# One PSUM tile or two for a head's attention scores, and a new fixed order of TensorE in the attention loop

## The chip, the cores and the metric

The kernel runs on one core of one Trainium2 chip. The metric is the device time of one execution in microseconds (us). A core has five engines that this text calls by the profile's names: PE (TensorE: matrix products and transposes; PEld is its weight load), DVE (VectorE), ACT (ScalarE), POOL (GpSimd) and SP (which issues DMAs here). In this kernel PE writes its results to tiles in PSUM, and DVE and ACT read them from there. [...] The engines work side by side and wait for one another by semaphores.

## What is computed

One layer of a hybrid block over 2048 latent tokens and 256 context tokens of width 1024: a modulated norm, one input projection, then two groups of heads side by side, an output projection, and a feed-forward part. The change lies in the stage in which both head groups are worked on. What it computes:

```python
keys = jnp.concatenate([kc, kx], axis=1)          # 256 + 2048 = 2304 keys
def block(q):                                     # 128 queries, 2 x 4 heads of 64
    s = jnp.einsum('bqkgd,bnkd->bkgqn', q, keys).astype(jnp.float32) * scale
    p = jax.nn.softmax(s, axis=-1)
    return jnp.einsum('bkgqn,bnkd->bqkgd', p.astype(vals.dtype), vals)
...
def step(S, inp):                                 # gated linear recurrence, 4 heads, two directions
    ...
    A = jnp.einsum('bhtk,bhsk,bhtsk->bhts', qc, kc, decay)
    o = jnp.einsum('bhts,bhsv->bhtv', A, vc) + jnp.einsum('bhtk,bhkv->bhtv', qc * jnp.exp(b), S)
```

## The kernel before

The kernel has three large stages: the norm and the input projection; the attention heads with the recurrence woven in; the output projection and the feed-forward part. Only the second stage is touched. PE's instructions there are issued in the order in which the program writes them (a manual schedule for PE alone, from the line `border.enter_context`). The instructions of DVE, ACT and POOL are put in order by the compiler's planner, which runs through the program on a model of the chip.

**Items.** The loop `for item in work` runs over 64 items: 2 key groups, 16 blocks of 128 queries, 2 pairs of heads. An item is a `Pair`: two heads of one block. Items overlap: while the scores of `cur` are made, the transposes and products of `prev` (the item before) are done, and `done` (the one before that) is finished.

**A head's scores.** `scores(hh, i)` handles one of two segments of the 2304 keys: segment 0 has 1536 keys, segment 1 has 768. PE writes the segment into PSUM (L814: 6 products of 512 columns for segment 0, 4 for segment 1, since each is the sum of two halves). DVE takes the minimum over each segment (L816; the queries carry the negated scale, so a minimum stands for the maximum), and over the two minima (L818). With segment 1, ACT then makes the exponentials of both segments into the SBUF tile `pr` (L822), each with a sum read out behind it. Before the change both segments lie in one PSUM tile `s_all` of 2560 columns, five banks, made once (L791) and written by every head.

**Transposes.** `transposes(k2)` (k2 from 0 to 8) turns two 128-column pieces of `pr` for both heads on PE (L831, four transposes) into a one-bank tile `pt` of the pool `ps_t2`, and copies it to the SBUF tile `pf`. The copy is on DVE (L835) for the k2 in `EV_DVE`, otherwise on ACT (L837). The pool has two banks.

**Products.** `products()` multiplies the nine `pf` tiles with the values (L844, 36 products, into one more tile of `ps_t2`), and ACT copies the result to `ot` (L848). `finish()` transposes `ot` on PE (L859, tile `pof`, also of `ps_t2`), and DVE divides by the sums (L861, L862, L864). POOL adds two halves (L866) and SP stores the block.

**The recurrence.** `other()` advances a generator `recurrence()`, which keeps two units of the other head group going in turn. A step is mostly one level of a tree: PE writes `pa` (L638), DVE merges it into `A` (L641), POOL makes the next `M`, `C` and `Q` (L650, L653, L662, L664), ACT copies parts (L656, L657), DVE makes the next `T` (L669). Other steps are `pd` (L627), transposes `pk` (L678) with copies on ACT (L680), `psf` and `psb` (L685, L697) with DVE's `S` (L692), and `po` (L728 to L730). All PSUM of the recurrence comes from `ps_h`, a pool of one bank. `STEPS / SLOTS` of a step is owed for each call, so that some calls advance nothing.

**The order.** One item issues its work to PE as `ORDER` says: -1 and -2 are segments 0 and 1 of the item's first head, -3 and -4 those of its second head; a positive number is so many transposes of `prev`; 0 is one call of `other()`. After the entry that leaves five transposes to do, `done.finish()` is called. `prev.products()` ends the item.

Of the kernel before, what the change touches and what calls it, by code (L numbers as in the profile page):

```python
# [9 lines left out]
F32 = mybir.dt.float32  # L10
F32R = mybir.dt.float32r
I32 = mybir.dt.int32
AF = mybir.ActivationFunctionType
ALU = mybir.AluOpType
AX = mybir.AxisListType

P = 128
# [25 lines left out]
DVE_MOD = (2, 5)  # L43
N_T, N_H = 2, 1
LIVE = 2
EV_DVE = (2, 5)
QI = WOE = "gpsimd"
STEPS = 4.4


ORDER = (-1, 2, 0, -2, 2, 0, 2, 0, 1, 0, -3, 2, -4, 0)
SLOTS = ORDER.count(0)

C_Q, C_K, C_HQ, C_I, C_FF, C_FB, C_G = 0, 512, 768, 1280, 1792, 2304, 2816
# [2 lines left out]
def rows_bcast(ap, n=P):  # L57

    return bass.AP(tensor=ap.tensor, offset=ap.offset, ap=[[0, n], [1, ap.size()]])
# [12 lines left out]
def block_kernel(ctx: ExitStack, tc: tile.TileContext, a: dict, out: bass.AP, dbg=None):  # L72
    nc = tc.nc
# [3 lines left out]
    def pool(stack, name, bufs=1, space=None, side=None):  # L77
        kw = dict(name=name, bufs=bufs, reuse_waits="tile", side=side)
        if space is not None:
            kw["space"] = space  # L80
        return stack.enter_context(tc.tile_pool(**kw))
# [67 lines left out]
    with ExitStack() as st:  # L149
# [36 lines left out]
        for r in range(2):  # L186
            for which in range(2):
                ks = slice(which * KT, (which + 1) * KT)
                nc.vector.tensor_tensor(modc[:, 2 * r + 1 - which, :], pcol[:, ks, r], bcol[:, ks],
                                        op=ALU.add)  # L190
# [21 lines left out]
    with ExitStack() as st:  # L212
# [39 lines left out]
        with ExitStack() as p1:  # L252
            ps_x = pool(p1, "ps_x", 4, PSUM)
            xh = pool(p1, "xh", 2)
            for gr in list(range(1, NTOK // 256)) + [0]:
# [7 lines left out]
                o = (gr - 1) % 2 * 256 if gr else 0  # L263
# [18 lines left out]
                for kk in range(KT // 2):  # L282
# [6 lines left out]
                    hh = xh.tile([P, 512], F32, tag="h", name=f"h{gr}_{kk}")  # L289
# [239 lines left out]
        for b in range(4):  # L529
            for gen, n in ((kv, 4 if b < 3 else 6), (hq, 2)):  # L530
                if b == 3 and gen is hq:
                    next(kv, 0)
                    w = load_w(steps[2][2])
# [6 lines left out]
        for i in range(2, len(steps)):  # L540
            f, c, _ = steps[i]
# [19 lines left out]
            w = wn  # L561
# [8 lines left out]
    with ExitStack() as st:  # L570
# [4 lines left out]
        op = pool(st, "op", 1, side="right")  # L575
# [3 lines left out]
        ps_s2 = pool(hst, "ps_s2", 1, PSUM)  # L579
# [208 lines left out]
        SEG = [(0, 1536), (1536, NTOK - 1536)]  # L788
        NSEG = len(SEG)
        NKT = NTOK // P  # L790
        s_all = ps_s2.tile([P, 2560], F32, name="s_all")  # L791

        class Pair:

# [7 lines left out]
            def scores(self, hh, i):  # L802


                nm = f"{self.nm}_{hh}"
                if i == 0:
                    self.negs.append(sm.tile([P, NSEG + 1], F32, tag="neg", name=f"neg{nm}"))
                neg = self.negs[hh]
                k0, n = SEG[i]
                for o, w in MM:  # L810
                    if not k0 <= o < k0 + n:
                        continue
                    for half in range(2):
                        nc.tensor.matmul(s_all[:, o:o + w], self.qs[:, hh, self.item[2], half, :],  # L814
                                         self.kv[0][:, o:o + w], start=(half == 0), stop=(half == 1))
                nc.vector.tensor_reduce(neg[:, i:i + 1], s_all[:, k0:k0 + n], axis=AX.X, op=ALU.min)  # L816
                if i == NSEG - 1:
                    nc.vector.tensor_reduce(neg[:, NSEG:], neg[:, :NSEG], axis=AX.X, op=ALU.min)  # L818
                    pr = pp.tile([P, NTOK], F32, tag="pr", name=f"pr{nm}")
                    self.prs.append(pr)  # L820
                    for j, (k0, n) in enumerate(SEG):
                        nc.scalar.activation(pr[:, k0:k0 + n], s_all[:, k0:k0 + n], AF.Exp,  # L822
                                             bias=neg[:, NSEG:], scale=-1.0,
                                             accum_out=self.ls[:, hh, j:j + 1])

            def transposes(self, k2):
# [6 lines left out]
                pf = self.pf[k2] = tp.tile([P, 512], F32, tag="pf", name=f"pf{self.nm}_{k2}")  # L833
                if k2 in EV_DVE:
                    nc.vector.tensor_copy(pf, pt)  # L835
# [34 lines left out]
        def load_kv(g):  # L870
            kv = (kvp.tile([P, NTOK], F32R, tag="K", name=f"K{g}"),
                  kvp.tile([P, NTOK // P, 64], F32, tag="V", name=f"V{g}"))
            nc.sync.dma_start(f32v(kv[0]), s_k[g])
            nc.sync.dma_start(kv[1], s_v[:, g * 64:(g + 1) * 64].rearrange("(t p) v -> p t v", p=P))
            return kv
# [5 lines left out]
        def other():  # L881

            nonlocal rec, debt
            debt += STEPS / SLOTS
            while debt >= 1 and rec is not None:
                debt -= 1
                if next(rec, 0) == 0:
                    rec = None
# [5 lines left out]
        for item in work + [None]:  # L894
            if item is None:
                while rec is not None:
                    other()
                order_T = iter(T_ORDER)
                for k2 in order_T:
                    prev.transposes(k2)  # L900
                    if done is not None:
                        done.finish()
                        done = None
                prev.products()
                prev.finish()
                border.close()
                hst.close()
                p5 = ctx.enter_context(ExitStack())
                wsp = pool(p5, "wsp", 3)
                wop = pool(p5, "wop")  # L910
                wo = [[wop.tile([P, D], F32R, name=f"wo{w}{k}") for w in "hl"] for k in range(KT)]
                gate1 = wop.tile([P, D], F32, name="gate1")
                mp = pool(p5, "mp", 2)
                ps_y = pool(p5, "ps_y", 2, PSUM)
                ps_mt = pool(p5, "ps_mt", 2, PSUM)
                for k in range(KT):
                    ws = wsp.tile([P, D], F32, tag="ws", name=f"wos{k}")
                    nc.sync.dma_start(ws, a["w_out"][0, k * P:(k + 1) * P, :])
                    nc.scalar.activation(wo[k][0], ws, AF.Copy)
                    (nc.vector if k in WOV else nc.gpsimd).tensor_tensor(  # L920
                        wo[k][1], ws, f32v(wo[k][0]), op=ALU.subtract)
                nc.sync.dma_start(gate1, rows_bcast(modrow[0, 2 * D:3 * D]))

                mixed = {}

                def mix_token(t):

                    rw = slice(t * P, (t + 1) * P)
                    mx = mp.tile([P, D], F32, tag="mix", name=f"mix{t}")
                    for g in range(2):  # L930
                        nc.sync.dma_start(mx[:, g * 256:(g + 1) * 256], s_att[g][rw, :])
                    for h in range(NH):
                        nc.sync.dma_start(mx[:, 512 + h * P:512 + (h + 1) * P], s_hg[h][rw, :])
                    mh = mp.tile([P, KT, P], F32R, tag="mh", name=f"mh{t}")
                    ml = mp.tile([P, KT, P], F32R, tag="ml", name=f"ml{t}")
                    for kk in range(2):
                        pt = ps_mt.tile([P, 512], F32, tag="t", name=f"mt{t}_{kk}")
                        for i in range(4):
                            k = kk * 4 + i
                            nc.tensor.transpose(pt[:, i * P:(i + 1) * P], mx[:, k * P:(k + 1) * P], ident)  # L940
                        pv = pt.rearrange("p (k t) -> p k t", t=P)
                        nc.scalar.activation(mh[:, kk * 4:kk * 4 + 4, :], pv, AF.Copy)
                        nc.vector.tensor_tensor(ml[:, kk * 4:kk * 4 + 4, :], pv,
                                                f32v(mh[:, kk * 4:kk * 4 + 4, :]), op=ALU.subtract)
                    mixed[t] = mh, ml

                mix_token(0)
                break
            qt, g, hp2 = item
            if (qt, hp2) == (0, 0):  # L950
                kv = load_kv(g)
            if hp2 == 0:
                qs = qpl.tile([P, 2, 2, 2, P], F32R, tag="qs", name=f"qs{qt}_{g}")
                nc.sync.dma_start(f32v(qs.rearrange("p h r a t -> p (h r a t)")),
                                  s_q[g][qt].rearrange("p h x -> p (h x)"))
            cur = Pair(item, kv, qs)
            todo = list(T_ORDER) if prev is not None else []
            for step in ORDER:
                if step < 0:
                    cur.scores((-step - 1) // NSEG, (-step - 1) % NSEG)  # L960
                elif step == 0:
                    other()
                else:
                    for _ in range(step):
                        if todo:
                            prev.transposes(todo.pop(0))
                    if len(todo) == 5 and done is not None:
                        done.finish()
            if prev is not None:
                prev.products()  # L970
            prev, done = cur, prev
# [4 lines left out]
    with ExitStack() as st:  # L976
# [88 lines left out]
        for pair in (1, 0):  # L1065
# [9 lines left out]
            for ff in range(NFF):  # L1075
                nm = f"{pair}_{ff}"
# [20 lines left out]
                hh = hid.tile([P, 1024], F32R, tag="hh", name=f"hh{nm}")  # L1097
# [104 lines left out]
```

## Time and profile before

| what | value |
|---|---|
| median of three runs | 3776.93 us (3775.04 to 3784.53) |
| profiled execution: its own time | 3772.86 us |
| profiled execution: its span | 3770.8 us |
| PE busy over the span | 3488.4 us (93%) |
| DVE, ACT, POOL busy over the span | 1665.1, 1284.5, 1086.9 us |
| first product of the scores (L814) starts | 724.8 us after the span's start |
| last one starts | 2071.3 us |

The span is cut below into the stretch before the attention loop (0 to 724), the loop (724 to 2076) and the rest. In the rows of instruction groups, the columns are: line, engine, operation, tiles written and read, shape and count; then the busy time in us and the mean of one in ns; then the idle time of that engine just before these instructions, with what ended most of it. In rows of the timeline the columns are start and duration in us, engine, line, operation, tiles, and in brackets the idle time of the engine before and what ended it. In rows of waits: who waited for whom, us in total, times, the longest.

### The profile page before, as it was taken

Reading aid. Unit: us, or ns where it says so; the run is one execution under the profiler, and the core shown is the slowest. Engines: PE = TensorE matmul, PEld = TensorE weight load, DVE = VectorE, ACT = ScalarE, POOL = GpSimd, SP = SyncE. Lnnn points to the kernel's source line nnn. Section 1 sums busy time; section 2 is a strip of 40 time slices with the busy share of each in tenths; the row PEclk is TensorE's granted clock in tenths of the full one; section 3 lists DMA queues with packets and bytes.
Section 4 is the critical chain, followed back from the end, with each engine's and each line's share of the span. In section 5 each row is a group of like instructions: output and inputs, shape, how many; then the busy total and the mean of one; then the engine's idle time right before and its main releaser. Section 6 shows DMA issues by size and latency. Waiting matters only on the chain.

```text
span 3770.8 us, 50158 instructions
## 1 busy us (share of the span) xinstructions
PE 3488.4 (93%) x19860; PEld 2864.0 (76%) x19860; DVE 1665.1 (44%) x2804; ACT 1284.5 (34%) x2363; POOL 1086.9 (29%) x1016
## 2 busy tenths in 40 slices
PE   8999999788888888888888999999999999999999
PEld 6999878766666666666666887888888888888887
DVE  6345553155545555454555454223232442323225
ACT  5322222256555555565655222111111121111112
POOL 4222222134324424341432013221222422122223
PEclk9999999899999999999999999999999999999999
DMA  7344554301020112001002353111111431111112
GB/s 234 97 131 143 171 173 143 118 20 35 29 59 24 32 52 57 23 27 51 24 15 89 124 213 101 51 51 39 51 45 56 158 111 45 45 56 45 45 51 84
DMA packets 279964, 293.94 MB, mean 78 GB/s; under 512 B 23120, under 2 KB 241200, under 8 KB 278448
## 3 DMA queue, kind: packets, MB, share of 16 engines
q1 hardware_dynamic: 279728, 290.73, 24.7%
q8 instruction: 156, 2.56, 0.3%
q14 instruction: 80, 0.66, 0.1%
HBM read 208.86 MB, written 81.81 MB: 77 GB/s over the span
## 4 chain that ended last, share of the span: by engine, by line
PE 69%; DVE 8%; ACT 3%; issue 2%; POOL 2%; DMA 1%; SPq 0%; DVEq 0%; POOLq 0%; ACTq 0%
PE pg L1105 26%; PE pd L1140 13%; PE s_all L814 7%; PE av L844 6%; DVE neg L816 6%; PE y L997 5%; PE i L351 3%; PE pa L638 2%; PE pt L831 2%; ACT pr L822 2%; ACT pf L837 1%; DMA F<-s_f 1%; POOL Q L664 1%; PE f L344 0%; POOL Q L662 0%
## 5 line engine op out<-in xcount | busy, mean ns | idle before, releaser
L816 DVE TENSOR_REDUCE neg<-s_all 128x1 f32<-128x1536 f32 (+1 forms) x256 | 347.2, 1356 | 281.1 <-PE s_all L814 280.8
L814 PE MATMUL s_all<-K,qs 128*128 128x512 f32 (+1 forms) x1280 | 340.9, 397 | 119.3 <-DVE neg L816 108.7
L814 PEld LDWEIGHTS s_all<-K,qs 128*128 128x128 f32 x1280 | 224.8, 191 | 208.3 <-DVE neg L816 138.6
L1112 DVE TENSOR_TENSOR sa<-pg,sa 128x512 f32<-128x512 f32 x88 | 60.8, 691 | 689.9 <-PE pg L1105 689.9
L1085 POOL TENSOR_TENSOR gl<-gs,gh 128x1024 fp32r<-128x1024 f32 x88 | 211.9, 2409 | 504.0 <-ACT gh L1084 503.8
L837 ACT ACTIVATE pf<-pt 128x512 f32<-128x512 f32 x448 | 253.8, 595 | 276.6 <-PE pt L831 275.9
L822 ACT ACTIVATE pr<-s_all,neg 128x1536 f32<-128x1536 f32 (+1 forms) x256 | 309.8, 1215 | 80.1 <-DVE neg L818 75.0
L831 PE MATMUL pt<-identr,pr 128*128 128x128 f32 x2304 | 311.6, 275 | 16.0 <-DVE pf L835 10.4
L1145 DVE TENSOR_TENSOR yy<-yy,pd 128x512 f32<-128x512 f32 x320 | 216.5, 684 | 207.9 <-PE pd L1140 207.5
L831 PEld LDWEIGHTS pt<-identr,pr 128*128 128x128 f32 x2304 | 264.9, 141 | 46.0 <-DVE pf L835 14.6
L1105 PE MATMUL pg<-h2h,gh 128*128 128x512 f32 x704 | 279.5, 397 | 0.0
L1105 PE MATMUL pg<-h2l,gh 128*128 128x512 f32 x704 | 279.4, 397 | 0.0
L1105 PE MATMUL pg<-h2lr,gh 128*128 128x512 f32 x704 | 279.1, 396 | 0.0
L1105 PE MATMUL pg<-h2hr,gl 128*128 128x512 f32 x704 | 279.0, 396 | 0.0
L1105 PE MATMUL pg<-h2hr,gh 128*128 128x512 f32 x704 | 279.0, 396 | 0.0
L1105 PE MATMUL pg<-h2h,gl 128*128 128x512 f32 x704 | 278.8, 396 | 0.0
L1140 PE MATMUL pd<-dl,hh 128*128 128x512 f32 x704 | 274.4, 390 | 0.0
L1140 PE MATMUL pd<-dh,hl 128*128 128x512 f32 x704 | 274.3, 390 | 0.0
L1140 PE MATMUL pd<-dh,hh 128*128 128x512 f32 x704 | 274.2, 389 | 0.0
L844 PE MATMUL av<-pf,V 128*64 128x256 f32 x2304 | 268.3, 388 | 0.0
L1095 POOL TENSOR_TENSOR dl<-ds,dh 128x1024 fp32r<-128x1024 f32 x44 | 107.7, 2448 | 497.8 <-ACT dh L1094 492.9
L1094 ACT ACTIVATE dh<-ds 128x1024 fp32r<-128x1024 f32 x44 | 46.7, 1062 | 544.5 <-PE pd L1140 466.1
(248 smaller groups left out, 7373.0 us busy)
## 6 DMA issues: line engine op xcount, KB each, us to landing
gs<-in_w_gu_dram SPq DMA_DIRECT2D x88, 512.0 KB
wm<-in_w_mod_dram SPq DMA_DIRECT2D x24, 1024.0 KB
ds<-in_w_down_dram SPq DMA_DIRECT2D x44, 512.0 KB
s_q<-sq SPq DMA_DIRECT2D x128, 128.0 KB
qs<-s_q SPq DMA_DIRECT2D x32, 512.0 KB
ws<-in_w_in_dram SPq DMA_DIRECT2D x9, 1024.0 KB
xt<-in_x_dram SPq DMA_DIRECT2D x16, 512.0 KB
s_f<-ft SPq DMA_DIRECT2D x16, 512.0 KB
```

Source lines behind the costliest of these rows:

```text
L351: nc.tensor.matmul(pm, hT[b][hi][:, k, j * P:(j + 1) * P], w[wi][:, k, :], start=(k == 0 and i == 0), stop=(k == KT - 1 and i == 2))
L814: nc.tensor.matmul(s_all[:, o:o + w], self.qs[:, hh, self.item[2], half, :], self.kv[0][:, o:o + w], start=(half == 0), stop=(half == 1))
L816: nc.vector.tensor_reduce(neg[:, i:i + 1], s_all[:, k0:k0 + n], axis=AX.X, op=ALU.min)
L822: nc.scalar.activation(pr[:, k0:k0 + n], s_all[:, k0:k0 + n], AF.Exp, bias=neg[:, NSEG:], scale=-1.0, accum_out=self.ls[:, hh, j:j + 1])
L831: nc.tensor.transpose(pt[:, (2 * i + hh) * P:(2 * i + hh + 1) * P], self.prs[hh][:, (2 * k2 + i) * P:(2 * k2 + i + 1) * P], ident)
L837: nc.scalar.activation(pf, pt, AF.Copy)
L844: nc.tensor.matmul(av[i * 64:(i + 1) * 64], self.kv[1][:, 2 * k2 + i, :], self.pf[k2][:, i * 256:(i + 1) * 256], start=(n == 0), stop=(n = ...
L997: nc.tensor.matmul(py, m[:, k, :], w[:, cs], start=(k == 0 and i == 0), stop=(k == KT - 1 and i == 2))
L1085: nc.gpsimd.tensor_tensor(wl, ws, f32v(wh), op=ALU.subtract)
L1105: nc.tensor.matmul(p, gws[ab][wi][:, k, :], h2[hf][xi][:, k, :], start=(k == 0 and i == 0), stop=(k == KT - 1 and i == 2))
L1140: nc.tensor.matmul(pd, l[:, ts_], r[:, cs], start=(i == 0), stop=(i == len(mm) - 1))
L1145: nc.vector.tensor_tensor(ys[j][:, cs], ys[j][:, cs], pd, op=ALU.add)
```

## The change

`s_all` is gone. `scores` allocates a new PSUM tile for each segment of each head: `s0` of 1536 columns (three banks) and `s1` of 1024 columns (two banks), each with a tag of its own and one buffer in the pool `ps_s2`, so that the five banks are the same in number. Three k2 (3, 4, 5) instead of two (2, 5) have their copy on DVE. `ORDER` has as many transposes and as many calls of `other()` as before, in other places, and `done.finish()` now stands in it as an entry of its own, 9.

```diff
-EV_DVE = (2, 5)
+EV_DVE = (3, 4, 5)
...
-ORDER = (-1, 2, 0, -2, 2, 0, 2, 0, 1, 0, -3, 2, -4, 0)
+ORDER = (-1, 2, -2, 2, 0, 2, 0, 9, 1, 0, 0, -3, 2, -4, 0)
...
-        s_all = ps_s2.tile([P, 2560], F32, name="s_all")
...
+                    self.s = []
                 neg = self.negs[hh]
                 k0, n = SEG[i]
+                s = ps_s2.tile([P, (1536, 1024)[i]], F32, tag=f"s{i}", name=f"s{i}_{nm}")
+                self.s.append(s)
...
-                        nc.tensor.matmul(s_all[:, o:o + w], self.qs[:, hh, self.item[2], half, :],
+                        nc.tensor.matmul(s[:, o - k0:o - k0 + w], self.qs[:, hh, self.item[2], half, :],
                                          self.kv[0][:, o:o + w], start=(half == 0), stop=(half == 1))
-                nc.vector.tensor_reduce(neg[:, i:i + 1], s_all[:, k0:k0 + n], axis=AX.X, op=ALU.min)
+                nc.vector.tensor_reduce(neg[:, i:i + 1], s[:, :n], axis=AX.X, op=ALU.min)
...
-                        nc.scalar.activation(pr[:, k0:k0 + n], s_all[:, k0:k0 + n], AF.Exp,
+                        nc.scalar.activation(pr[:, k0:k0 + n], self.s[j][:, :n], AF.Exp,
...
+                elif step == 9:
+                    if done is not None:
+                        done.finish()
...
-                    if len(todo) == 5 and done is not None:
-                        done.finish()
```

## The prediction

> **What bounds the kernel now.** The page comes first: where the span goes, and what the chain that ended last is made of.
>
> ```profile
> PE 3488.4 (93%) x19860; PEld 2864.0 (76%) x19860; DVE 1665.1 (44%) x2804; ACT 1284.5 (34%) x2363; POOL 1086.9 (29%) x1016
> ...
> PE pg L1105 26%; PE pd L1140 13%; PE s_all L814 7%; PE av L844 6%; DVE neg L816 6%; PE y L997 5%; PE i L351 3%; PE pa L638 2%; PE pt L831 2%; ACT pr L822 2%; ACT pf L837 1%; DMA F<-s_f 1%; POOL Q L664 1%; PE f L344 0%; POOL Q L662 0%
> ```
>
> PE is the bound, but DVE's minimum L816 holds 6% of the chain: PE is waiting for it. The view by windows says where (columns: stretch, length, then busy us of PE, PEld, DVE, ACT, POOL, the granted clock, DMA share, GB/s).
>
> ```profile
> 0.00:724.00 724.00, 699.73 (x4643) 621.73 (x4644) 331.81 (x867) 206.37 (x448) 188.57 (x164) 0.99 0.49 150
> 724.00:2076.00 1352.00, 1105.89 (x7787) 872.04 (x7786) 723.35 (x1161) 754.48 (x1437) 487.01 (x650) 0.98 0.14 41
> 2076.00:3770.80 1694.80, 1682.73 (x7434) 1370.20 (x7432) 609.92 (x777) 323.69 (x479) 411.36 (x202) 1.00 0.23 76
> ```
>
> PE idles 24.3 us before the attention loop, 12.1 us behind it, and 1352.0 - 1105.9 = 246.1 us in it. No other engine is busy for 60% of the loop, so this idle time is made of waits in an order, not of a second full engine. The instruction groups of PE in the loop share it out:
>
> ```profile
> L814 PE MATMUL s_all<-K,qs 128*128 128x512 f32 (+1 forms) x1280 | 340.9, 397 | 119.3 <-DVE neg L816 108.7 <-ACT pr L822 6.0 <-issue 1.7
> L831 PE MATMUL pt<-identr,pr 128*128 128x128 f32 x2272 | 307.3, 275 | 16.0 <-DVE pf L835 10.4 <-DVE neg L818 2.5 <-ACT pf L837 1.6
> ...
> L638 PE MATMUL pa<-Q,M 128*128 128x128 f32 x896 | 130.5, 290 | 28.2 <-POOL Q L664 9.9 <-DVE S L692 4.8 <-ACT kt L680 4.3
> L859 PE MATMUL pof<-identr,ot 128*128 128x128 f32 x124 | 27.1, 300 | 44.0 <-ACT pf L837 44.0
> ...
> L627 PE MATMUL pd<-q,kk 128*128 128x128 f32 x128 | 18.5, 290 | 16.1 <-POOL kk L621 13.4 <-ACT kt L680 2.0 <-DVE A L641 0.4
> ```
>
> Three parts: the scores 119.3; transposes and `pof` 16.0 + 44.0 = 60.0; the rest, 246.1 - 179.3 = 66.8, is the recurrence, of which 13.4 is a single wait. The timeline shows how the first two come about.
>
> ```profile
> 1440.93 4.11 PE L844 MATMUL av<-pf,V 128*64 128x256 f32 x36
> ...
> 1441.14 0.15 DVE L818 TENSOR_REDUCE neg<-neg 128x1 f32<-128x2 f32 x1
> ...
> 1444.97 1.66 PE L814 MATMUL s_all<-K,qs 128*128 128x512 f32 x6
> ...
> 1446.46 1.03 PE L831 MATMUL pt<-identr,pr 128*128 128x128 f32 x8
> 1446.66 1.76 DVE L816 TENSOR_REDUCE neg<-s_all 128x1 f32<-128x1536 f32 x1 [2.23 <-PE s_all L814]
> ...
> 1448.47 0.97 PE L814 MATMUL s_all<-K,qs 128*128 128x512 f32 x4 [0.53 <-DVE neg L816]
> ...
> 1451.00 0.44 PE L859 MATMUL pof<-identr,ot 128*128 128x128 f32 x2 [0.69 <-ACT pf L837]
> ...
> 1452.79 0.75 DVE L641 COPY_PREDICATED A<-mask,pa 128x512 f32<-128x512 int32 x1 [0.89 <-PE pa L638]
> ...
> 1453.59 0.52 PEld L697 LDWEIGHTS psb<-V,kt 128*128 128x128 f32 x4 [0.21 <-DVE A L641]
> ```
>
> Segment 1 starts at 1448.47, 0.05 after DVE ends its minimum over segment 0 (1446.66 + 1.76 = 1448.42). It writes other columns than DVE reads there. So the wait belongs to the tile as a whole, and with one tile for both segments every segment 1 pays it: the minimum takes 1.76, and the eight transposes between cover about 0.9 of that.
>
> **The change part by part.** The rows that price it, by shape, first DVE, then ACT:
>
> ```profile
> L816 DVE TENSOR_REDUCE neg<-s_all 128x1 f32<-128x1536 f32 x128 | 224.7, 1756 | 177.5 <-PE s_all L814 177.3
> L816 DVE TENSOR_REDUCE neg<-s_all 128x1 f32<-128x768 f32 x128 | 122.5, 957 | 103.6 <-PE s_all L814 103.5
> L835 DVE COPY pf<-pt 128x512 f32<-128x512 f32 x126 | 86.3, 685 | 33.0 <-PE pt L831 30.2
> L641 DVE COPY_PREDICATED A<-mask,pa 128x512 f32<-128x512 int32 x112 | 83.4, 744 | 55.9 <-PE pa L638 55.5
> ```
>
> ```profile
> L837 ACT ACTIVATE pf<-pt 128x512 f32<-128x512 f32 x441 | 249.7, 595 | 267.5 <-PE pt L831 266.7
> L822 ACT ACTIVATE pr<-s_all,neg 128x1536 f32<-128x1536 f32 x128 | 196.9, 1538 | 80.1 <-DVE neg L818 75.0 <-PE po L730 2.7
> L822 ACT ACTIVATE pr<-s_all,neg 128x768 f32<-128x768 f32 x128 | 114.2, 892 | 0.0
> L822 ACT ACTIVATION_READ_ACCUMULATOR pr<-s_all,neg 128x1 f32 x256 | 50.3, 197 | 0.0
> ```
>
> *Two tiles.* The wait on segment 0's minimum goes. In its place `s0` waits until ACT has made the exponentials of the head before, `s1` likewise. Is that in time? Counted from the end of the second head's segment 0: two transposes (1.03) and segment 1 (0.97) end at 2.0; minima to 2.0 + 0.96 + 0.15 = 3.1; first exponential and its sum to 3.1 + 1.54 + 0.20 = 4.85, about 5.0 with handovers. PE comes back for the next `s0` after 2.0 + 4.11 of products = 6.1 at the earliest: a cover of 1.1 us. `s1` is needed later still. If DVE or ACT is more than 1.1 us late, PE stops there, and transposes, `pof` and recurrence behind it stop too. I leave 10 us of the 119.3: **-109**. Bounds: 2 left (as the 1.7 of issue), or 40 (a third, if the cover breaks often).
>
> [...]
>
> *`pof` and the transposes.* Today `pof` stands right behind two transposes and waits for a copy (595 ns on ACT) in 62 of 62 cases. Now it stands behind one call of `other()`, about 1.2 of PE work where there is any (130.5 / 112 for a level). How often is there? From the program: 112 steps `pa` (896 / 8 in the row), 16 `pd` (128 / 8), 80 with `pk`, `psf` or `psb`, 16 `po`: 224 of 64 x 5 = 320 calls, 70%. In the other 30%, 19 items, `pof` waits as today, 0.7 each: 13 us. The copies 3, 4, 5 on DVE: copy 3 comes up 1.03 us after segment 1 ends, and DVE is done with segment 1's minimum 1.0 us after it, so it fits just so. Where no call stands between, copies 3 and 5 are late by 0.4 and 0.25: 12 us; 5 more for odd cases. 60.0 becomes 30: **-30**. Bounds: 15 left, or all 60.
>
> Engine load is no obstacle: 64 copies of 685 ns make DVE's 723 us 767, ACT falls to 716, both far below the loop.
>
> *The calls of `other()`.* As many as before, but two stand together (`0, 0`), and the place between the first head's segments loses one. The pool `ps_h` has one bank: the second of a pair waits until DVE has emptied it. In the timeline `psb` (1453.59) starts 0.05 after L641 ends (1452.79 + 0.75), although eight transposes stood between. Without cover that is 0.84 us a pair, against 0.5 less today with four transposes between. Pairs that both hold PE work: 0.7 x 0.7 x 63 = 31, so +16. Also, three narrow gaps stand in an item now (eight transposes; `pof` and four; none) where two did; the two cost (66.8 - 13.4) = 53.4 today, so one more is +27. POOL makes four products a level and must keep up in the burst:
>
> ```profile
> L662 POOL TENSOR_TENSOR Q<-Q,T 128x256 f32<-128x256 f32 x96 | 66.6, 693 | 190.5 <-PE pa L638 190.4
> ```
>
> Four of 0.7 are 2.8 us a level, and each of the two units is asked again two calls later, after about 3 us (a call of 1.2, and one of 1.0 to 1.2 or the work between): just enough. Sum **+43**. Bounds: 0 (the narrow gaps only move), and 31 x 2.3 + 27 = 98, if each pair costs the longest wait seen:
>
> ```profile
> PE pa L638 <- POOL Q L664: 9.9, 8, 2.3
> ```
>
> The sum: -109 - 30 + 43 = -96, on the profiled execution's own 3772.86 (span 3770.8, 2.1 around it): 3677. The median of the runs, 3776.93, lies 4.1 above that execution, so as a median **3681**.
>
> **The rivals.** *Little comes back:* the narrow gaps cost what they cost today, 2 and 15 us are left of the others: -117 - 45 = -162, median 3615. For it: DVE and ACT have 45% of the loop free. Against it: one bank for a pair of calls.
>
> *DVE's order:* copies 3, 4 and 5 queue behind minima, `A` and `T`. If each item loses one short minimum (0.96) so, 63 x 0.96 = 60 comes back: -36, median 3741. For it: those copies fit only just. Against it: `pt` waited for DVE's copies only 10.4 us with two of them. [...]
>
> *The wait stays (slower):* if segment 1 still waits for segment 0's minimum, the first head has lost the call that covered it. All 128 segments then wait 1.0: 128 against 119.3 now, +9; with -30 and +43 that is +22, median 3799. It decides once less than 13 of the 119.3 us go. Against it: two tiles have nothing in common.
>
> **How the numbers follow.** A run can tell about 0.3%, 11 us, from no change. Forecast (60 to 130 us gained, 3647 to 3717) 0.58; little comes back (3600 to 3647) 0.17; DVE's order (11 to 60 gained) 0.14; within 11 us, by the bounds of the three terms meeting, 0.04; slower 0.07. So faster 0.89, same 0.04, slower 0.07. The range leaves out the best 0.05 of the second case, 0.03 of the third, and the last two, 0.19 in all: 3624 to 3755.
>
> **What would show it.** Right: the loop shrinks from 1352 to about 1256 and the stretches around it don't change; L814's idle time is near 10 us with DVE's L816 gone as its releaser; L859 and L831 together idle about 30; the recurrence's lines about 110, more of it ended by DVE's L641 or POOL; L835 runs 192 times. Wrong: L814 still idle behind L816 (the wait stays), L831 and `pof` idle 80 or more behind L835 (DVE's order), or recurrence lines under 75 (little comes back). A changed time outside the loop would be none of these.

## The result, and the profile after

The changed kernel takes 3644.54 us (median of four runs, 3638.36 to 3652.36), the kernel before 3775.98 us in the same comparison. The ratio is 0.9649, 95% interval [0.9624, 0.9674]: 131 us faster, where 96 were forecast. That lies in the range, but in the part of it that the prediction gave to the rival "little comes back".

The view by windows of the changed kernel, cut where its loop ends (columns as in the prediction):

```profile
0.00:724.00 724.00, 702.54 (x4654) 623.17 (x4654) 332.36 (x870) 208.31 (x449) 189.32 (x164) 0.99 0.50 151
724.00:1937.00 1213.00, 1086.61 (x7770) 877.41 (x7770) 743.07 (x1219) 714.54 (x1365) 480.58 (x648) 0.96 0.15 44
1937.00:3636.60 1699.60, 1684.24 (x7440) 1370.18 (x7436) 618.11 (x782) 328.92 (x485) 417.37 (x204) 1.00 0.24 77
```

The span fell by 134.2 us. The windows have fixed edges, while the first product of the scores starts at 720.0 us in the changed kernel, at 724.8 in the kernel before and up to 732.3 in the runs below, so that a window holds a few us of other work, or misses some. From the first product of the scores to the end of the last one, the loop is 133.6 us shorter (1346.7 to 1213.1): PE's idle time gave 117.6 (245.6 to 128.0) and its busy time 16.1 (1101.1 to 1085.0). The prediction had no term for the second. Busy times that are compared below are taken in this way. The granted clock in the loop is lower than before, 0.96 against 0.98: by the trace's clock records PE's clock is at half for 85.3 us of the loop, where it was 61.4.

The groups of PE's instructions in that window; scores are now L817, transposes L834, `pof` L862, and the rest are lines of the recurrence:

```profile
L817 PE MATMUL s<-K,qs 128*128 128x512 f32 x1270 | 345.5, 404 | 6.8 <-ACT pr L825 5.4 <-ACT ot L851 1.3
L834 PE MATMUL pt<-identr,pr 128*128 128x128 f32 x2268 | 310.8, 277 | 14.3 <-ACT pf L840 6.6 <-DVE pf L838 4.9 <-DVE neg L821 2.4
...
L639 PE MATMUL pa<-Q,M 128*128 128x128 f32 x896 | 133.7, 294 | 43.8 <-POOL Q L665 17.0 <-DVE S L693 9.1 <-DVE A L642 7.3
L729 PE MATMUL po<-V,A 128*128 128x128 f32 x128 | 27.1, 296 | 7.5 <-DVE o L746 5.6 <-DVE neg L821 1.8
...
L862 PE MATMUL pof<-identr,ot 128*128 128x128 f32 x124 | 25.3, 286 | 7.8 <-DVE pf L838 7.7
L698 PE MATMUL psb<-V,kt 128*128 128x128 f32 x144 | 22.8, 305 | 9.2 <-DVE S L693 6.4 <-DVE A L642 2.0 <-ACT dS L701 0.8
L686 PE MATMUL psf<-V,kt 128*128 128x128 f32 x144 | 20.9, 287 | 9.0 <-ACT kt L681 3.2 <-ACT A L629 3.0 <-DVE A L642 1.6
L628 PE MATMUL pd<-q,kk 128*128 128x128 f32 x128 | 19.4, 299 | 20.2 <-POOL kk L622 16.3 <-ACT kt L681 1.9 <-DVE A L642 1.2
L679 PE MATMUL pk<-identr,C 128*128 128x128 f32 x72 | 18.6, 281 | 5.6 <-ACT kt L681 4.6 <-DVE A L642 1.0
L679 PE MATMUL pk<-identr,M 128*128 128x128 f32 x72 | 18.5, 280 | 3.9 <-DVE A L642 2.7 <-ACT kt L681 1.2
```

The scores wait 6.8 us instead of 119.3, and no longer for DVE's minimum: most of what is left waits for ACT's exponentials (5.4). Transposes and `pof` idle 22.1 instead of 60.0. The seven rows of the recurrence add up to 99.2 instead of 66.8. One item in PE's own timeline:

```profile
1481.35 1.66 PE L817 MATMUL s<-K,qs 128*128 128x512 f32 x6
1482.85 1.03 PE L834 MATMUL pt<-identr,pr 128*128 128x128 f32 x8
1483.64 0.96 PE L817 MATMUL s<-K,qs 128*128 128x512 f32 x4
1484.44 1.04 PE L834 MATMUL pt<-identr,pr 128*128 128x128 f32 x8
1485.72 1.25 PE L834 MATMUL pt<-identr,pr 128*128 128x128 f32 x8 [0.25 <-ACT pf L840]
1486.81 1.13 PE L639 MATMUL pa<-Q,M 128*128 128x128 f32 x8
1487.78 0.38 PE L862 MATMUL pof<-identr,ot 128*128 128x128 f32 x2
1488.00 0.60 PE L834 MATMUL pt<-identr,pr 128*128 128x128 f32 x4
1489.72 1.16 PE L639 MATMUL pa<-Q,M 128*128 128x128 f32 x8 [1.12 <-POOL Q L665]
1493.85 2.07 PE L639 MATMUL pa<-Q,M 128*128 128x128 f32 x8 [2.97 <-POOL Q L665]
1495.58 2.91 PE L817 MATMUL s<-K,qs 128*128 128x512 f32 x6
```

Segment 1 (1483.64) has no bracket: it starts on the heels of the transposes, and even overlaps the last of them (1482.85 + 1.03 = 1483.88). Further down stand the two neighbouring calls of the recurrence, with 1.12 and 2.97 us of waiting, and behind them rows that take nearly twice their usual time (2.07 for 1.13, 2.91 for 1.66). The last section comes back to those.

### The profile page after: what moved, and what is told of

It is laid out like the page before. It is cut to its first block, busy times and chain, and to the rows that moved or that the text cites. A ratio compares the mean times of both kernels' runs of the same rounds, so it can differ in the third digit from the quotient of the medians.

```text
span 3636.6 us, 50114 instructions
## 1 busy us (share of the span) xinstructions
PE 3473.4 (96%) x19860; PEld 2870.8 (79%) x19860; DVE 1693.5 (47%) x2868; ACT 1251.8 (34%) x2299; POOL 1087.3 (30%) x1016
## 5 line engine op out<-in xcount | busy, mean ns | idle before, releaser
L819 DVE TENSOR_REDUCE neg<-s 128x1 f32<-128x1536 f32 (+1 forms) x256 | 338.1, 1352 | 152.8 <-PE s L817 152.4
L817 PE MATMUL s<-K,qs 128*128 128x512 f32 (+1 forms) x1280 | 347.8, 403 | 6.8 <-ACT pr L825 5.4
L825 ACT ACTIVATE pr<-s,neg 128x1536 f32<-128x1536 f32 (+1 forms) x256 | 309.7, 1215 | 73.2 <-DVE neg L821 73.1
L834 PE MATMUL pt<-identr,pr 128*128 128x128 f32 x2304 | 316.2, 277 | 17.2 <-ACT pf L840 6.6
L834 PEld LDWEIGHTS pt<-identr,pr 128*128 128x128 f32 x2304 | 265.2, 142 | 57.0 <-DVE pf L838 13.8
L840 ACT ACTIVATE pf<-pt 128x512 f32<-128x512 f32 x384 | 216.3, 596 | 213.9 <-PE pt L834 213.5
L817 PEld LDWEIGHTS s<-K,qs 128*128 128x128 f32 x1280 | 232.2, 198 | 68.7 <-ACT pr L825 14.3
## 6 DMA issues: line engine op xcount, KB each, us to landing
s_q<-sq SPq DMA_DIRECT2D x128, 128.0 KB
```

The costliest lines, as they stand in the source:

```text
L817: nc.tensor.matmul(s[:, o - k0:o - k0 + w], self.qs[:, hh, self.item[2], half, :], self.kv[0][:, o:o + w], start=(half == 0), stop=(half = ...
L819: nc.vector.tensor_reduce(neg[:, i:i + 1], s[:, :n], axis=AX.X, op=ALU.min)
L825: nc.scalar.activation(pr[:, k0:k0 + n], self.s[j][:, :n], AF.Exp, bias=neg[:, NSEG:], scale=-1.0, accum_out=self.ls[:, hh, j:j + 1])
L834: nc.tensor.transpose(pt[:, (2 * i + hh) * P:(2 * i + hh + 1) * P], self.prs[hh][:, (2 * k2 + i) * P:(2 * k2 + i + 1) * P], ident)
L840: nc.scalar.activation(pf, pt, AF.Copy)
```

## The experiments

Two theories stood against each other. The first, the prediction's: the wait belongs to the tile, so two tiles bring the gain, and the order brings `pof` forward but pays for its pair of calls. The second: the order does the work, by putting other work of PE under each wait. All times are medians of four runs; a ratio is to the kernel before in the same comparison.

**Tiles alone.** The changed kernel with the old order and the old copies:

```diff
-EV_DVE = (3, 4, 5)
+EV_DVE = (2, 5)
-ORDER = (-1, 2, -2, 2, 0, 2, 0, 9, 1, 0, 0, -3, 2, -4, 0)
+ORDER = (-1, 2, 0, -2, 2, 9, 0, 2, 0, 1, 0, -3, 2, -4, 0)
```

> Two tiles alone: the order of TensorE and the copies on VectorE (2, 5) as before the change. Theory (the wait belongs to the tile): the scores' idle time falls from 119 us to under 10, pof keeps about 44 and the transposes about 16, the recurrence rises from 67 to 70 or 75; with about 95 stalls fewer, each of which also costs some 0.19 us of overlap of neighbouring matmuls, 3776 - 112 - 18 + 5 = about 3650 us. Rival (the new order does most of it, by putting the waits under other work): scores still idle over 50 us, and over 3700 us.

Measured: 3635.75 us, ratio 0.9627 [0.9612, 0.9643]. The window of its loop and two groups of PE:

```profile
724.00:1935.00 1211.00, 1067.93 (x7806) 865.29 (x7806) 716.89 (x1159) 749.38 (x1432) 482.33 (x649) 0.98 0.16 45
```

```profile
L817 PE MATMUL s<-K,qs 128*128 128x512 f32 (+1 forms) x1280 | 338.2, 395 | 11.2 <-ACT pr L825 9.9 <-ACT ot L851 1.3
...
L862 PE MATMUL pof<-identr,ot 128*128 128x128 f32 x124 | 27.1, 300 | 46.0 <-ACT pf L840 42.5 <-DVE neg L821 3.5
```

The scores' wait is gone, `pof` keeps its own. The two tiles alone bring as much as the whole change: the intervals overlap, so a difference between 0.9627 and 0.9649 is not shown.

**Order and copies alone**, with the one tile `s_all`. The diff is that of the change without its two tiles.

> The new order and the copies 3, 4, 5 on VectorE alone, with the one tile of before. Theory: every segment 1 waits for segment 0's minimum, 128 x 1.0 = 128 us; pof and transposes fall from 60 to about 25, the recurrence rises from 67 to about 99: 3776 + 9 - 35 + 32 = about 3780 us, between 3765 and 3800. Rival (the order does most of it): under 3740 us.

Measured: 3807.87 us, ratio 1.0088 [1.0068, 1.0108], slower than before.

```profile
L814 PE MATMUL s_all<-K,qs 128*128 128x512 f32 (+1 forms) x1280 | 350.5, 405 | 147.0 <-DVE neg L816 137.0 <-ACT pr L822 7.9 <-ACT ot L848 1.4
```

So the second theory falls. Without the second tile, segment 1 waits for the minimum in 127 of its 128 cases, where it was 95 in the old order, and the kernel is 33 us slower than before. The wait was larger than the 128 expected, and the time some 8 us above the expected stretch.

**The pair taken apart:**

```diff
-ORDER = (-1, 2, -2, 2, 0, 2, 0, 9, 1, 0, 0, -3, 2, -4, 0)
+ORDER = (-1, 2, -2, 2, 0, 2, 0, 9, 1, 0, -3, 2, 0, -4, 0)
```

> The changed kernel with the two neighbouring calls of the recurrence taken apart: the second one is moved between the second head's two transposes and its segment 1. Theory (a pair costs 0.84 us, since one PSUM bank serves both): idle time in the recurrence's lines falls from 99 us to about 85, and the time from 3644 to about 3630 us. Rival (the recurrence's own chain over VectorE, ScalarE and GpSimd is late, wherever the calls stand): recurrence within 5 us of 99, time within 6 us of 3644.

Measured: 3611.97 us, ratio 0.9566 [0.9551, 0.9582], clear of the changed kernel's 0.9649 [0.9624, 0.9674].

```profile
724.00:1907.00 1183.00, 1075.92 (x7823) 867.58 (x7821) 744.94 (x1221) 712.25 (x1367) 479.83 (x648) 0.98 0.16 46
```

Moving one call saves 33 us, more than twice what was expected. From the first to the last product of the scores the loop is 39.1 us shorter (1213.1 to 1174.0): 21.0 less idle time (128.0 to 107.0) and 18.0 less busy time (1085.0 to 1067.0), while the time at half clock falls from 85.3 to 41.0 us. The stretch ahead of the loop, which the order does not touch, took 8.8 us longer in this trace.

**The old copies in the new order:**

```diff
-EV_DVE = (3, 4, 5)
+EV_DVE = (2, 5)
```

> The changed kernel with the copies 2 and 5 on VectorE, as before the change, so that copy 4 is on ScalarE. Theory (ScalarE makes the exponentials of the first head just then, about 3 us of work, and copy 4 queues behind them): pof and transposes idle 60 us or more instead of 25, 3680 us. Rival (the planner puts copy 4 ahead of the exponentials, and the choice of copies matters little): pof and transposes under 35, time within 10 us of 3644.

Measured: 3682.16 us, ratio 0.9755 [0.9736, 0.9773]. ACT and DVE in one item of its timeline:

```profile
1429.73 1.09 PE L834 MATMUL pt<-identr,pr 128*128 128x128 f32 x8 [0.69 <-ACT pf L840]
...
1429.95 1.54 ACT L825 ACTIVATE pr<-s,neg 128x1536 f32<-128x1536 f32 x1 [0.27 <-DVE neg L821]
...
1431.48 0.89 ACT L825 ACTIVATE pr<-s,neg 128x768 f32<-128x768 f32 x1
...
1432.36 0.59 ACT L840 ACTIVATE pf<-pt 128x512 f32<-128x512 f32 x1
1432.38 0.41 DVE L867 TENSOR_TENSOR oo<-pof,li 128x256 f32<-128x256 f32 x1
...
1432.85 0.66 PE L834 MATMUL pt<-identr,pr 128*128 128x128 f32 x4 [0.80 <-DVE oo L867]
```

Copy 4 belongs to the transposes at 1429.73, but ACT makes it at 1432.36, behind both exponentials. Its bank stays full until then, and the next transposes take the bank of `pof`: they wait 0.80 us, until DVE has divided it. Over the whole loop:

```profile
L834 PE MATMUL pt<-identr,pr 128*128 128x128 f32 x2268 | 309.0, 277 | 59.6 <-DVE oo L867 37.7 <-ACT pf L840 20.4 <-DVE pf L838 1.4
```

Transposes and `pof` idle 59.6 + 21.5 = 81.1 us instead of 22.1. With the old copies the new order is some 38 us slower than with copies 3, 4 and 5 on DVE; other choices were not run.

**The same copies in the old order**, with two tiles:

```diff
-EV_DVE = (2, 5)
+EV_DVE = (3, 4, 5)
 ORDER = (-1, 2, 0, -2, 2, 9, 0, 2, 0, 1, 0, -3, 2, -4, 0)
```

> Two tiles and the old order, with the copies 3, 4, 5 on VectorE instead of 2 and 5. Theory (pof takes the bank whose copy ends first; copy 2 is now on ScalarE and begins half a microsecond before copy 3 would): pof's idle time falls from 46 us to under 20, 3636 - 28 = about 3607 us. Rival (what helped pof was only its later place): pof stays over 35 us, time within 8 us of 3636.

Measured: 3621.64 us, ratio 0.9595 [0.9580, 0.9610]; tiles alone had 0.9627.

```profile
L862 PE MATMUL pof<-identr,ot 128*128 128x128 f32 x124 | 27.2, 301 | 20.1 <-ACT pf L840 16.1 <-DVE neg L821 3.5 <-DVE neg L819 0.5
```

`pof` idles 20.1 us instead of 46.0 without having been moved. The time fell by 14 us only, half of what was expected.

**`finish` one call later, and then the calls spread out:**

```diff
-ORDER = (-1, 2, 0, -2, 2, 9, 0, 2, 0, 1, 0, -3, 2, -4, 0)
+ORDER = (-1, 2, 0, -2, 2, 0, 9, 2, 0, 1, 0, -3, 2, -4, 0)
...
+ORDER = (-1, 2, 0, -2, 2, 0, 9, 2, 0, 1, -3, 0, 2, -4, 0)
```

> The same, with finish one call of the recurrence later. Theory: pof idles under 8 us, transposes about 15, recurrence about 71 as with the tiles alone: about 3595 us. Rival (the order costs through something else than the neighbouring calls): over 3620 us.

> As the one with finish later, and the fourth call behind the second head's segment 0, so that at least 1.5 us of other work of TensorE lies between any two calls. Theory (the recurrence waits where calls stand close, and nowhere else): its idle time falls from 71 us to 60 or less, of which 16 are the start; granted clock at half for 40 us of the loop or less; about 3580 us. Rival (its own chain is late wherever the calls stand): 70 us or more, time as with finish later.

Measured: 3593.77 us, ratio 0.9518 [0.9501, 0.9535], and 3576.64 us, ratio 0.9473 [0.9459, 0.9487]. Both theories hold in time. In the parts the first has misses, partly in opposite directions: transposes rose from 15.8 to 28.9 instead of staying near 15, `pof` idles 9.7 instead of under 8, and the recurrence 61.9 instead of about 71. The spread order brings the recurrence to 46.1 us:

```profile
L639 PE MATMUL pa<-Q,M 128*128 128x128 f32 x896 | 131.1, 291 | 20.1 <-DVE S L693 8.7 <-POOL Q L665 5.1 <-DVE A L642 3.6
```

Of the 46.1, 16.2 is the one wait at the start (`pd`). Where the calls stand apart, the rest is 29.9 us over the whole loop. The clock is at half for 37.5 us of it.

**Three calls side by side**, to see whether the price of a pair grows:

```diff
-ORDER = (-1, 2, -2, 2, 0, 2, 0, 9, 1, 0, 0, -3, 2, -4, 0)
+ORDER = (-1, 2, -2, 2, 0, 2, 9, 1, 0, 0, 0, -3, 2, -4, 0)
```

> The changed kernel with three calls of the recurrence side by side instead of two. Theory of the waits alone: one more pair of 0.84 to 1.6 us in half of the items, recurrence from 99 to about 145 us, 3644 + 46 = 3690 us. Theory that bunched waits cost a second time through the clock (a stretch of 3.4 us in which TensorE is busy for less than half of it is followed by 3.4 us at half clock): the same idle time, half clock for 130 us or more of the loop instead of 89, and 3710 us or more.

Measured: 3681.67 us, ratio 0.9752 [0.9731, 0.9773]. Both theories miss.

```profile
L639 PE MATMUL pa<-Q,M 128*128 128x128 f32 x896 | 135.0, 296 | 46.4 <-POOL Q L665 17.4 <-DVE A L642 12.7 <-DVE S L693 7.3
L862 PE MATMUL pof<-identr,ot 128*128 128x128 f32 x124 | 27.1, 300 | 22.4 <-DVE pf L838 22.3
```

The recurrence idles 105.0 us, hardly more than 99.2. `pof` idles 22.4 instead of 7.8, since it lost the call ahead of it, and PE's busy time in the loop rose by 14.3 us (1085.0 to 1099.3). The clock is at half for 99.0 us of the loop against 85.3, where the second theory expected 130 or more. By its clock records, the changed kernel's loop has 18 steps of 3.41 us at full clock in which PE is busy for less than half: 17 are followed by half clock (in the kernel before, 11 of 15). A third call beside two mostly trades one narrow gap for another, so this run does not give the price of a pair.

**The spread order with `finish` late, and, without that move, with one tile:**

```diff
-ORDER = (-1, 2, 0, -2, 2, 0, 9, 2, 0, 1, -3, 0, 2, -4, 0)
+ORDER = (-1, 2, 0, -2, 2, 0, 2, 0, 9, 1, -3, 0, 2, -4, 0)
```

> The even order with finish where the changed kernel has it, behind the third pair of transposes and a call. Theory (transposes now idle 33 us because copies 4 and 5 need the bank that pof still holds until VectorE has divided it): transposes near 17 us, pof near 8, about 3558 us. Rival (VectorE is late either way, behind the minima): transposes and pof together 40 us or more, time within 6 us of 3577.

> The even order and the copies 3, 4, 5 with the one tile of before. Theory (the wait belongs to the tile, and a call between the segments covers it where the call holds work): scores idle 50 to 90 us, the rest as with two tiles, 3577 + 65 + 10 of lost overlap = about 3650 us. Rival (an order that puts a call between the segments of both heads makes the second tile needless): scores under 25 us, under 3600 us.

Measured: 3569.21 us, ratio 0.9464 [0.9449, 0.9480], and 3684.32 us, ratio 0.9762 [0.9743, 0.9781]. The first can't be told from the 0.9473 without the move; transposes and `pof` fell from 31.6 + 7.7 to 24.1 + 3.1, between the two expectations. The second has the order of the first line of the diff, with `s_all` in place of the two tiles:

```profile
L814 PE MATMUL s_all<-K,qs 128*128 128x512 f32 (+1 forms) x1280 | 342.2, 398 | 95.1 <-DVE neg L816 71.5 <-ACT pr L822 18.9 <-issue 1.5
```

Even with a call between the segments of both heads, one tile costs 95.1 us of waiting against 6.4, and 3684 against 3577 us. That was 34 us more than expected.

PE's idle time in the loop, us, from the groups as above (recurrence: its rows added up). PE busy and the time at half clock, from the trace's clock records, are taken from the first to the last product of the scores:

| kernel | scores | transposes | `pof` | recurrence | PE busy | half clock | time |
|---|---|---|---|---|---|---|---|
| before | 119.3 | 16.0 | 44.0 | 66.8 | 1101.1 | 61.4 | 3776 |
| changed | 6.8 | 14.3 | 7.8 | 99.2 | 1085.0 | 85.3 | 3645 |
| tiles alone | 11.2 | 14.5 | 46.0 | 71.3 | 1061.2 | 41.0 | 3636 |
| order and copies alone | 147.0 | 13.0 | 8.8 | 97.1 | 1116.0 | 88.7 | 3808 |
| pair apart | 5.1 | 15.8 | 7.6 | 78.4 | 1067.0 | 41.0 | 3612 |
| spread | 6.4 | 31.6 | 7.7 | 46.1 | 1052.7 | 37.5 | 3577 |
| spread, `finish` late | 6.5 | 24.1 | 3.1 | 50.6 | 1051.2 | 34.1 | 3569 |

## Why the prediction was right, and where it was off

**The wait belongs to the tile: right.** Shown three times, with the tile as the only difference: in the old order (119.3 to 11.2), in the new one (147.0 to 6.8), in the spread one (95.1 to 6.4). The step's size, -109, came out at -112.5. The 1.1 us of cover for the exponentials held: only 5.4 us of waits for ACT are left.

**`pof` and the transposes: right, a little too small.** -30 was forecast, -37.9 came (60.0 to 22.1). The prediction gave it to the later place and to copies that fit only just. Both count: in the old order the copies alone took `pof` from 46.0 to 20.1 and the later place then to 9.7, and in the new order the old copies give 81.1 us of waiting. The rival "DVE's order" is refuted: PE waits 4.9 + 7.7 us for DVE's copies, far from the idle time of 80 that was named as its sign.

**The calls of `other()`: right in kind, one term mis-sized.** +43 was forecast, +32.4 came. Within it the pair was priced at 16 and the third narrow gap at 27. With the pair apart, the recurrence with three narrow gaps idles 78.4 against 71.3 with the two of the old order, or 76.1 in the old order with the same copies: 7 us or less, not 27. The pair cost 20.8 (99.2 - 78.4), and the two tiles alone added 4.5 (66.8 to 71.3). So the sum was near by luck: two errors offset each other in part. Taking half of all the recurrence's waits as the price of one gap was the mistake: those waits depend on how far apart the calls stand (99.2 in the changed order, 46.1 in the spread one).

**What the sum did not hold.** PE's busy time fell by 16.1 us, and the sum had no term for it. Two things in the traces go with it. By the profile, which models the ends of matmuls, a matmul group that didn't wait began before the last one ended, by 0.24 us in the changed kernel (1483.64 against 1483.88) and 0.17 in the kernel before (1446.46 against 1446.63); behind an idle gap there is no such overlap. And at a granted clock of 0.50 six products of the scores took 2.91 us, where they took 1.66 at 1.00. Between the first and the last product of the scores, PE has 300 idle gaps before, 183 in the changed kernel and 181 with tiles alone. Over the loops of all twelve kernels, PE's busy time (1051 to 1116 us) is met within 3.3 us by 1002 + 0.25 for each gap + 0.41 for each us at half clock. By this estimate the change gained 29 us through fewer gaps and gave back 10 through the clock. Between tiles alone and the whole change the gaps are the same in number, and 44.3 us more at half clock make up 18 of the 23.8 us of busy time. It is a fit: no run changes one of the two alone.

**The rival "little comes back"** has the measured time in its part, but not by its mechanism: its sign was recurrence lines under 75, and they came to 99.2. The loop went beyond the forecast because each of the three terms came out better, 22 us together (-112.5, -37.9 and +32.4 make -118.0 for -96), and because of the 16.1 us of busy time.

**The rival "the wait stays"** was a kernel that could be run: the order with one tile. Its price of 22 us came out at 33.

The whole change is therefore two tiles that bring all of the gain, and an order, with its copies, that brought nothing that can be measured when put on top of them. In that order the gain at `pof` (46.0 to 7.8) was given back at the recurrence (71.3 to 99.2) and in PE's busy time (1061.2 to 1085.0).

## What to carry to other kernels

If an engine waits for a reader of columns that it isn't going to write, look at which tile holds them: a wait can belong to the tile and not to the data. Here none of three orders removed it (119.3, 147.0 and 95.1 us left), while a second tile in the same number of banks did (11.2, 6.8 and 6.4 left). When an order written by hand is changed together with a buffer, run the two halves alone; here one half brought everything and the other had a better variant 2% faster. The calls of the recurrence, which need a chain over other engines and share one PSUM bank, waited least where the order had them farthest apart (46.1 us, against 99.2 with two side by side), so that is worth a run of its own.

## What the runs showed of the hardware

Behind the two neighbouring calls of the changed kernel PE's granted clock falls from 1.00 to 0.50. The changed kernel in stretches of 3.4 us around the two calls shown in the timeline (the second number is the length, the first busy time is PE's, the granted clock stands behind the five engines):

```profile
1485.60:1489.00 3.40, 2.88 (x22) 2.46 (x22) 3.04 (x7) 2.71 (x6) 0.97 (x2) 1.00 0.00 0
1489.00:1492.40 3.40, 1.16 (x8) 0.97 (x8) 1.42 (x3) 1.76 (x4) 3.40 (x5) 1.00 0.07 19
1492.40:1495.80 3.40, 1.95 (x9) 1.95 (x10) 0.71 (x1) 0.00 (x0) 2.62 (x5) 0.50 0.02 5
1495.80:1499.20 3.40, 3.40 (x12) 2.71 (x12) 2.44 (x3) 0.90 (x2) 3.10 (x4) 0.50 0.01 2
1499.20:1502.60 3.40, 3.40 (x29) 2.82 (x29) 2.19 (x3) 2.26 (x4) 0.00 (x0) 0.99 0.03 10
```

PE is busy for 1.16 of 3.40 us, a third, and the clock is at 0.50 in the next stretch. That one holds 1.95 of 3.40 busy, and the half clock goes on for another. In these two stretches, six products of the scores take 2.91 us instead of 1.66. At another place one such stretch was enough, with PE busy for nearly half of it:

```profile
1209.10:1212.50 3.40, 1.62 (x11) 1.46 (x12) 0.73 (x2) 2.14 (x6) 1.68 (x4) 1.00 0.38 96
1212.50:1215.90 3.40, 3.40 (x13) 2.92 (x12) 1.34 (x2) 0.88 (x2) 3.18 (x6) 0.50 0.00 0
```

No single idle gap of PE fills such a stretch (2.97 us is the longest of those shown, 0.98 and 0.82 those around 1210), so the stretches are sorted here by PE's busy share in them. The clock records of the twelve traces change in steps of 3.41 us. Cut into such steps, the loops have 82 at full clock in which PE is busy for less than 0.45: each is followed by half clock. Of 209 with 0.45 to 0.60, 38 are, and of 3814 with more, none. Over the whole span the mean clock is 0.985 in the changed kernel and 0.991 with the pair apart: twice the missing share, (1 - 0.985) x 2 x 3636.6 = 109 us and (1 - 0.991) x 2 x 3607.9 = 65 us at half clock. So waits that stand together cost a second time in these kernels: the four kernels with neighbouring calls have 71.7 to 99.0 us of half clock in the loop, the eight others 34.1 to 61.4. This, and a pair price of 20.8 us where 14 was expected, accounts for most of what taking the pair apart saved beyond the expected 14: PE was busy for 18.0 us less, with 44.3 us less of half clock. The run with three calls, meant to show it by size, had only 13.7 us more of half clock than the changed kernel, so how the price grows is not shown.
